# One layer of a streaming encoder on one core: x and its norm weight loaded in four column groups, cached keys loaded one set ahead, the conv state's output spread out

## The chip, the core and the metric

One core of a Trainium2 chip runs the whole program: TensorE (PE, with its weight loads as PEld), VectorE (DVE), ScalarE (ACT), GpSimd (POOL) and SyncE (SP), which issues most of the DMAs. POOL issues the others. The metric is the time of the program on the device in microseconds (us). Three runs of the kernel before took 3035.05, 3035.47 and 3037.78 us, median 3035.47.

## The reference

The program is one layer, applied to a prompt of 512 positions and a sample of 64 positions with 1024 cached ones. Model width is 2048, all in fp32.

```python
h = rmsnorm(x, norm_w) * (1.0 + scale[:, None]) + shift[:, None]
proj = h @ w_in                                   # 18032 columns, split into the parts below
conv_out, conv_new = causal_conv(qkv_a, conv_prev, w_conv)   # conv_new is an output: 3 rows x 6144
o_a, S_new = gated_delta_rule(qa, ka, va, g, beta, S0)       # 16 heads of 128
y_a = (rmsnorm(o_a, gdn_norm_w) * silu(z_a)) @ w_branch_a
o_b = sparse_attention(q_b, q_i, w_i, pos, K, V, KI, topk, rel_bias)  # 16 heads, 2 sets of keys
y_b = (o_b * silu(z_b)) @ w_branch_b
merged = sigmoid(gl_a) * y_a + sigmoid(gl_b) * y_b
x = x + gate[:, None] * (merged @ w_out)
y = rmsnorm(x, final_norm_w)                      # prompt and sample
```

For the sample, K and V are the cached keys and values (`cache_k`, `cache_v`, 1024 positions, 2 sets of 128 columns) followed by the new ones.

## The kernel before

The work is a stream of 189 tiles of 128 columns of a weight matrix (`plan`, line 1706): first the columns of `w_in`, then `w_branch_a`, `w_branch_b` and `w_out`. A tile is 96 products of 128x128 by 128x288: the activations and the weights are split into a high and a low part (`whi`, `wlo`; `hh` and `hl` for h, `ga`, `gb`, `mg` later), and hi·hi, hi·lo and lo·hi are summed, for two halves (288 columns each) of the 576 positions. Tile n's products first take the 64 with `whi`, then the 32 with `wlo` (`run_tile`, line 314). While tile n runs, ACT splits the weights of tile n+1, in four pieces at products 4, 14, 24 and 34; the low part is finished by a DMA that POOL issues (`wlo <- wraw`, it adds the raw weights to the negated high part). At product 84 SP issues the load of tile n+3's raw weights (`wraw`, 1 MB in rows of 512 bytes). There are two buffers each of `wraw`, `whi` and `wlo`, so that a load of `wraw` waits on SP for POOL's transfer out of the same buffer.

Between the products stands the rest of the work: attention, recurrence, transposes, each written as a generator. The planner (`Plan`, line 70) keeps an estimate of PE's time in ns (`self.pe`) while the program is written out. After each product `tick` steps every task whose due time has come. A `yield` says when a task is due again: a number is so many ns of PE's time from now, a list of tiles is when these are estimated to be ready, a tuple of a list and a number is that plus so many ns, `None` is at once; `wait` polls other tasks every 200 ns. The estimate only decides the order in which instructions are written. On the chip each engine takes its own instructions in that order, and waits at each for what it reads and for its buffer. So a PE instruction that waits holds all products behind it, and a DMA on SP's queue holds all DMAs behind it.

Three places matter here.
- `open_att` (line 1779) is called at the first tile of the queries (`qb0`). It closes the buffers of the recurrence and opens a pool in the same memory. It spawns `conv_out` (line 1310), which transposes the new conv state on PE (`nc`), copies it on DVE (`ncr`, two buffers) and stores it; `gate_vectors`, which loads `gada`, 256 KB in rows of 2 KB, over and over; and `kv_load(0)` (line 1323).
- `kv_load(n)` loads set n's keys and values: `KT` and `V` of the new positions, then 1024 cached values, and the cached keys in two parts of 512 (`kst`, one buffer, 256 KB in rows of 512 bytes), which PE transposes (`kcp`) and DVE copies (`KC`). Set 1 is loaded when head 8 of 16 begins (`qb_pre`, line 1446).
- `open_final` (line 1814) is called at the first tile of `w_out`. It loads x (4 MB for the prompt, 0.5 MB for the sample) and the final norm's weight (`fw`, 1 MB, spread over the partitions). The tiles' epilogue `wo_epi` scales the sums by the gate on ACT (`og`), and `out_cols` (line 1657) transposes them on PE (`yp`, `yq`, in two buffers of PSUM that all transposes share), adds them to x on DVE (`xf`), takes squares on ACT (`fscr`) and multiplies by `fw` on DVE.

Tiles are called by their order: `qb0` is the first one of the queries, `wo0` the first one of `w_out`, and `wlo174` is the low part for tile 174. All DVE, ACT, POOL and SP instructions go through the helper at line 58, products through line 221 and transposes through line 236.

Of the kernel before, what the change touches and what calls it, by code (L numbers as in the profile page):

```python
# [7 lines left out]
F32 = mybir.dt.float32  # L8
# [200 lines left out]
class Kern(Plan):  # L209
# [54 lines left out]
    def load(self, n):  # L264
        if n >= len(self.stream):
            return
        d = self.stream[n]
        m = d["m"] = sum(w for _, _, w in d["srcs"])
        raw = d["raw"] = self.wp.tile([128, 2048], F32, tag="wraw", name=f"wraw{n}")
        r3 = raw[:, :KO * m].rearrange("p (k m) -> p k m", m=m)  # L270
        at = 0
        for src, c, w in d["srcs"]:
            self.S.dma_start(r3[:, :, at:at + w], src[:, c:c + w].rearrange("(k p) m -> p k m", p=128))
            at += w
# [1035 lines left out]
    def conv_out(self):  # L1310
        o, p = self.o, self.p3
        f = self.newc.rearrange("p a b -> p (a b)")
        for g, name in enumerate(("prompt", "sample")):
            dst = o["new_conv_" + name].rearrange("l b j (m p) -> (l b j m) p", p=128)
            for a, n in ((0, 96), (96, 48)):
                pt = yield from self.tr(f"nc{g}{a}")
                self.T32(pt[:n, :128], f[:, 144 * g + a:144 * g + a + n])
                r = p.tile([128, 128], F32, tag="ncr", name=f"ncr{g}{a}")
                self.V.tensor_copy(r[:n], pt[:n, :128])
                yield [r]  # L1320
                self.S.dma_start(dst[a:a + n], r[:n])

    def kv_load(self, n):
        i, p, S = self.i, self.p3, self.S
        KT = p.tile([128, T], F32, tag="KT", name=f"KT{n}", bufs=1)
        S.dma_start(KT, self.d_kT[n])
        V = p.tile([128, 13, 128], F32, tag="V", name=f"V{n}", bufs=1)
        S.dma_start(V[:, 0:4, :], self.d_v[0:TP, 128 * n:128 * n + 128].rearrange("(t p) c -> p t c", p=128))
        S.dma_start(V[:64, 12, :], self.d_v[TP:T, 128 * n:128 * n + 128])
        S.dma_start(V[:, 4:12, :], i["cache_v"][0, 0, :, n, :].rearrange("(t p) c -> p t c", p=128))  # L1330
        KC = p.tile([128, PAST], F32, tag="KC", name=f"KC{n}", bufs=1)
        self.kvs = (KT, KC, V)
        for g in range(2):
            k = p.tile([128, 4, 128], F32, tag="kst", name=f"kst{n}{g}", bufs=1)
            S.dma_start(k, i["cache_k"][0, 0, 512 * g:512 * g + 512, n, :].rearrange("(t p) c -> p t c", p=128))
            yield [k]
            pt = yield from self.tr(f"kcp{n}{g}")
            for t in range(4):
                self.T32(pt[:, 128 * t:128 * t + 128], k[:, t, :])
            self.V.tensor_copy(KC[:, 512 * g:512 * g + 512], pt)  # L1340
            yield None
        yield [V, KT, KC]

    def attend(self, a):
# [9 lines left out]
    def attend_block(self, a, t, BT):  # L1354

        V, A, p, h = self.V, self.A, self.p3, a["h"]
        KT, KC, VV = self.kvs
        sc = 128 ** -0.5
# [5 lines left out]
        pl = yield from self.tp(f"lg{h}{t}")  # L1364
        self.mm(pl[:, :nk], a["qT"][:, q], KT[:, :nk])
        L = p.tile([128, nk], F32, tag=f"L{t}", name=f"L{h}{t}", bufs=1)
# [30 lines left out]
    def attend_sample(self, m):  # L1397
        V, A, S, p = self.V, self.A, self.S, self.p3
        KT, KC, VV = self.kvs
        sc = 128 ** -0.5  # L1400
# [238 lines left out]
    def wo_epi(self, j):  # L1639
# [14 lines left out]
                self.spawn(self.finish((0, 1), self.cols[KO - 2], self.cols[KO - 1]))  # L1654
        return epi

    def out_cols(self, j, g, ts):

        V, A, p, x = self.V, self.A, self.p8, self.x
        c = slice(128 * j, 128 * j + 128)  # L1660
        yield [g]
        full = [t for t in ts if t < 4]
        a, b = full[0], full[-1] + 1
        pt = yield from self.tr(f"yp{j}_{a}")
        for t in full:
            self.T32(pt[:, 128 * t:128 * t + 128], g[:, 128 * t:128 * t + 128])
        V.tensor_tensor(x[:, a:b, c], pt[:, 128 * a:128 * b].rearrange("p (a b) -> p a b", b=128), x[:, a:b, c], op=ALU.add)
        if 4 in ts:
            pt = yield from self.tr(f"yq{j}")
            self.T32(pt[:64, :128], g[:, TP:])  # L1670
            V.tensor_tensor(x[:64, 4, c], pt[:64, :128], x[:64, 4, c], op=ALU.add)
        yield 900
        for t in ts:
            n = 128 if t < 4 else 64
            scr = p.tile([128, 128], F32, tag="fscr", name=f"fscr{j}{t}")
            A.activation(scr[:n], x[:n, t, c], AF.Square, accum_out=self.sq[:n, t, j:j + 1])
        if j < KO - 1:
            yield 1500
            V.tensor_tensor(x[:, a:b, c], x[:, a:b, c], self.fw[:, c].unsqueeze(1).to_broadcast([128, b - a, 128]), op=ALU.mult)
            if 4 in ts:  # L1680
                V.tensor_tensor(x[:64, 4, c], x[:64, 4, c], self.fw[:64, c], op=ALU.mult)
# [132 lines left out]
    def open_final(self):  # L1814
        self.drain()
        self.cgb.close()
        self.c8, p = self.pool("p8", side="left")
        self.p8 = p
        i, S = self.i, self.S
        self.og, self.cols = {}, {}  # L1820
        self.x = p.tile([128, 5, D], F32, name="xf", bufs=1)
        S.dma_start(self.x[:, 0:4, :], i["x_prompt"][0].rearrange("(t p) d -> p t d", p=128))
        S.dma_start(self.x[:64, 4, :], i["x_sample"][0])
        self.fw = p.tile([128, D], F32, name="fw", bufs=1)
        S.dma_start(self.fw, i["final_norm_w"].partition_broadcast(128))
        self.sq = p.tile([128, 5, KO], F32, name="sqf", bufs=1)
        self.V.memset(self.sq[64:128, 4, :], 1.0)

# [113 lines left out]
```

## Time and profile before

| | |
|---|---|
| median of three runs | 3035.47 us |
| the profiled execution's own time | 3037.4 us |
| its span, first to last instruction | 3035.6 us |
| PE busy | 2938.0 us, 97% of the span |
| PEld busy | 2824.9 us, 93% |
| DVE, ACT, POOL busy | 40%, 50%, 13% |
| mean granted clock of TensorE | 0.986 of full speed |
| DMA, mean | 184 GB/s |

PE is busy nearly always, but the shares are a mean over stages. In the views by time a row begins with its start and its length in us; what stands in brackets at its end is how long the engine stood before it, and for what. A granted clock of 1.00 is the upper of TensorE's two levels (2.4 GHz), 0.50 the lower (1.2 GHz). q1 is the queue of SP's DMAs, q0 that of POOL's; after the name stand packets, MB, and the time that they took as a share of 16 DMA engines.

### The profile page before, as it was taken

To read this page: it belongs to the slowest core of one execution; us is meant where nothing else is said; L and a number is where in the kernel's file an instruction comes from. 1 tells how busy PE (TensorE), PEld (TensorE's weight loads), DVE (VectorE), ACT (ScalarE), POOL (GpSimd) and SP (SyncE) were. 2 spreads that over 40 slices of the span, in tenths; PEclk is the share of its full clock that TensorE was granted. 3 is DMA by queue.
4 is the path that set the end of the run, shared out by engine and by line. 5 is a ranking of instruction groups with operands and counts; after the bars stand their busy time and mean duration, and the time that the engine had idled before them with its cause. 6 is when DMAs were issued, how large, how long until landed. Compare 5 with 4: busy or idle time off the path is not lost.

```text
span 3035.6 us, 59288 instructions
## 1 busy us (share of the span) xinstructions
PE 2938.0 (97%) x23931; PEld 2824.9 (93%) x23931; DVE 1205.0 (40%) x3643; ACT 1531.8 (50%) x3428; POOL 399.3 (13%) x792
## 2 busy tenths in 40 slices
PE   5999999999999999999999999899999999999897
PEld 2599999999999999999999999899999999999897
DVE  3344896544454455544542434244322111112112
ACT  3266445555555555655554545354544443344454
POOL 1011111111111111111111111000111111111110
PEclk7999999999999999999999999999999999999999
DMA  9875887667677666767768677777679889888875
GB/s 326 273 162 125 188 191 183 158 161 177 154 164 168 157 161 155 172 163 173 168 158 191 164 165 179 177 168 167 151 171 263 231 223 225 217 204 213 217 160 139
DMA packets 571379, 558.84 MB, mean 184 GB/s; under 512 B 55121, under 2 KB 465650, under 8 KB 569890
## 3 DMA queue, kind: packets, MB, share of 16 engines
q1 hardware_dynamic: 515794, 354.69, 40.8%
q0 software_dynamic: 55168, 200.30, 34.5%
q8 instruction: 188, 3.08, 0.4%
q14 instruction: 85, 0.70, 0.1%
q10 hardware_dynamic: 144, 0.07, 0.0%
HBM read 313.52 MB, written 47.48 MB: 119 GB/s over the span
## 4 chain that ended last, share of the span: by engine, by line
PE 82%; DMA 10%; ACT 3%; DVE 2%; SPq 2%; issue 1%; POOL 0%; ACTq 0%; DVEq 0%; POOLq 0%
PE mm L221 66%; DMA yl<-d_ya 2%; SPq L58 2%; DMA za<-d_za 2%; DMA wlo<-wraw 1%; DMA wa<-in_w_ada 1%; DMA gbl<-d_gb 1%; PE ob L221 1%; PE lg L221 1%; PE ada L221 1%; PE po L221 1%; PE mmp L221 1%; PE dot L221 1%; DMA xf<-in_x_sample 1%; ACT wlo L58 1%
## 5 line engine op out<-in xcount | busy, mean ns | idle before, releaser
L221 PE MATMUL mm<-hh,whi 128*128 128x288 f32 (+1 forms) x4448 | 1223.8, 301 | 3.9 <-ACT gth L58 3.7
L221 PE MATMUL mm<-hl,whi 128*128 128x288 f32 (+1 forms) x4448 | 1221.2, 300 | 0.0
L221 PEld LDWEIGHTS mm<-hh,whi 128*128 128x128 f32 (+1 forms) x4448 | 838.0, 188 | 13.8 <-ACT gth L58 4.2
L221 PEld LDWEIGHTS mm<-hl,whi 128*128 128x128 f32 (+1 forms) x4448 | 838.4, 188 | 8.2 <-issue 3.8
L221 PE MATMUL mm<-hh,wlo 128*128 128x288 f32 (+1 forms) x4448 | 685.1, 302 | 0.0
L221 PEld LDWEIGHTS mm<-hh,wlo 128*128 128x128 f32 (+1 forms) x4448 | 615.4, 189 | 1.9 <-issue 0.9
L58 POOL DMA_DIRECT2D wlo<-wraw x376 | 323.2, 860 | 2231.9 <-ACT wlo L58 1875.4
L58 ACT ACTIVATE whi<-wraw 128x512 fp32r<-128x512 f32 x756 | 467.3, 618 | 96.9 <-DMA wraw<-in_w_branch_b 61.0
L58 ACT ACTIVATE wlo<-whi 128x512 fp32r<-128x512 f32 x752 | 475.2, 632 | 77.2 <-PE mm L221 37.3
L221 PE MATMUL mm<-ga,whi 128*128 128x288 f32 x1024 | 141.9, 299 | 8.2 <-DVE ta L58 8.2
L221 PEld LDWEIGHTS mm<-ga,whi 128*128 128x128 f32 x1024 | 139.5, 191 | 8.9 <-DVE ta L58 8.9
L221 PE MATMUL mm<-mg,whi 128*128 128x288 f32 x1024 | 144.0, 298 | 0.0
L221 PE MATMUL mm<-gb,whi 128*128 128x288 f32 x1024 | 139.9, 296 | 0.6 <-DVE tb L58 0.6
L221 PEld LDWEIGHTS mm<-mg,whi 128*128 128x128 f32 x1024 | 138.7, 189 | 0.0
L221 PEld LDWEIGHTS mm<-gb,whi 128*128 128x128 f32 x1024 | 137.5, 188 | 1.3 <-DVE tb L58 1.3
L58 DVE SCALAR_TENSOR_TENSOR cv<-raw,cw,cv 128x579 f32<-128x579 f32 x144 | 117.9, 818 | 27.8 <-ACT cv L58 24.2
L58 DVE SCALAR_TENSOR_TENSOR gacc<-gada,cs,gacc 128x512 f32<-128x512 f32 x120 | 86.2, 744 | 3.2 <-DMA gada<-in_w_ada 3.2
L58 ACT ACTIVATE raw<-mm 128x288 f32<-128x288 f32 x96 | 36.7, 382 | 82.9 <-PE mm L221 82.1
L58 ACT ACTIVATE gth<-mm 128x288 f32<-128x288 f32 x64 | 25.9, 407 | 103.7 <-PE mm L221 102.5
L58 ACT ACTIVATE x<-px 128x128 f32<-128x128 f32 x80 | 21.9, 273 | 107.7 <-PE px L221 107.7
L58 DVE TENSOR_TENSOR xf<-yp,xf 128x512 f32<-128x512 f32 (+1 forms) x18 | 11.4, 632 | 161.7 <-PE yp L236 134.0
L58 DVE SCALAR_TENSOR_TENSOR tb<-tb,mm 128x288 f32<-128x288 f32 x32 | 14.5, 453 | 144.3 <-DMA tb<-d_t 105.1
(494 smaller groups left out, 3437.8 us busy)
## 6 DMA issues: line engine op xcount, KB each, us to landing
wlo<-wraw POOLq DMA_DIRECT2D x376, 512.0 KB, 5.4
wraw<-in_w_in SPq DMA_DIRECT2D x140, 1024.0 KB
wa<-in_w_ada SPq DMA_DIRECT2D x64, 512.0 KB
gada<-in_w_ada SPq DMA_DIRECT2D x64, 256.0 KB
wraw<-in_w_branch_a SPq DMA_DIRECT2D x16, 1024.0 KB
wraw<-in_w_branch_b SPq DMA_DIRECT2D x16, 1024.0 KB
wraw<-in_w_out SPq DMA_DIRECT2D x16, 1024.0 KB
d_t<-gth SPq DMA_DIRECT2D x32, 288.0 KB
```

The costliest lines, as they stand in the source:

```text
L58: r = f(*a, **k)
L221: self.nc.tensor.matmul(out, lhsT, rhs, start=start, stop=stop, **k)
```

## The change

Three parts of the program are edited; nothing else differs.

1. `x_in` (new) loads x and `fw` in four groups of 512 columns. Group g waits until the task of group g-1 is done, which is 14 us of the planner's time after its loads were issued. `out_cols` for column tile j waits for the tasks of the groups before its own, and for every fourth tile its transposes are due 2 us later than before.
2. `kv_load` issues the load of the first cached keys before all its other loads, and that of the next part as soon as the one buffer is free, so that set 1's first part is loaded right after set 0's second. Transposes are due 4 us after the estimated landing, except for set 1's first part, which is due at once.
3. `conv_out` waits 24 us of the planner's time ahead of each of its four pieces.

```diff
@@ conv_out
             for a, n in ((0, 96), (96, 48)):
+                yield 24000
                 pt = yield from self.tr(f"nc{g}{a}")
@@ kv_load
+        def load(m, g):
+            k = p.tile([128, 4, 128], F32, tag="kst", name=f"kst{m}{g}", bufs=1)
+            S.dma_start(k, i["cache_k"][0, 0, 512 * g:512 * g + 512, m, :].rearrange("(t p) c -> p t c", p=128))
+            return k
+        k = load(0, 0) if n == 0 else self.kst
         KT = p.tile([128, T], F32, tag="KT", name=f"KT{n}", bufs=1)
...
         for g in range(2):
-            k = p.tile([128, 4, 128], F32, tag="kst", name=f"kst{n}{g}", bufs=1)
-            S.dma_start(k, i["cache_k"][0, 0, 512 * g:512 * g + 512, n, :].rearrange("(t p) c -> p t c", p=128))
-            yield [k]
+            yield [k], 4000 * (g or 1 - n)
...
             yield None
+            if n + g < 2:
+                k = self.kst = load(n + g, 1 - g)
@@ new
+    def x_in(self, g):
+
+        S, i, c = self.S, self.i, slice(512 * g, 512 * g + 512)
+        if g:
+            yield from self.wait(self.xl[g - 1])
+        S.dma_start(self.x[:, 0:4, c], i["x_prompt"][0][:, c].rearrange("(t p) d -> p t d", p=128))
+        S.dma_start(self.x[:64, 4, c], i["x_sample"][0][:, c])
+        S.dma_start(self.fw[:, c], i["final_norm_w"][c].partition_broadcast(128))
+        yield 14000
@@ out_cols
-        yield [g]
+        yield from self.wait(*self.xl[:j // 4])
+        yield [g], 0 if j % 4 else 2000
@@ open_final
-        S.dma_start(self.x[:, 0:4, :], i["x_prompt"][0].rearrange("(t p) d -> p t d", p=128))
-        S.dma_start(self.x[:64, 4, :], i["x_sample"][0])
         self.fw = p.tile([128, D], F32, name="fw", bufs=1)
-        S.dma_start(self.fw, i["final_norm_w"].partition_broadcast(128))
+        self.xl = []
+        for g in range(4):
+            self.xl.append(self.spawn(self.x_in(g)))
```

SP's queue where the first set of keys is loaded (`qb0`), before; `d_t` is the store of a gate tile, `kst01` the second part of set 0:

```order
L58 DMA d_t_85<-gth15_20000 128x576
L58 DMA gada0_20042<-in_w_ada 128x512
L58 DMA gada1_20044<-in_w_ada 128x512
L58 DMA KT0_20048<-d_kT_80 128x576
L58 DMA V0_20050<-d_v_81 128x4x128
L58 DMA V0_20050<-d_v_81 64x128
L58 DMA V0_20050<-in_cache_v 128x8x128
L58 DMA kst00_20055<-in_cache_k 128x4x128
L58 DMA out_new_conv_prompt<-ncr00_20040 96x128
```

The same place now:

```order
L58 DMA d_t_85<-gth15_20000 128x576
L58 DMA gada0_20038<-in_w_ada 128x512
L58 DMA gada1_20040<-in_w_ada 128x512
L58 DMA kst00_20044<-in_cache_k 128x4x128
L58 DMA KT0_20046<-d_kT_80 128x576
L58 DMA V0_20048<-d_v_81 128x4x128
L58 DMA V0_20048<-d_v_81 64x128
L58 DMA V0_20048<-in_cache_v 128x8x128
L58 DMA wraw98_20154<-in_w_in 128x16x128
L58 DMA kst01_20164<-in_cache_k 128x4x128
```

`kst00` has moved ahead of `KT0` and `V0`, the four conv stores are gone from here, and `kst01` follows the weight load.

PE at the end of that tile, before; the tile's 64 products with `whi` and the four `nc` transposes stand ahead of these rows:

```order
L221 MATMUL mm95_0_20036<-hh_105,wlo95_19887 128x288 x10
L236 MATMUL kcp00_0_20161<-ident_60,kst00_20055 128x128 x4
L221 MATMUL mm95_0_20036<-hh_105,wlo95_19887 128x288 x6
L221 MATMUL mm95_1_20113<-hh_105,wlo95_19887 128x288 x16
L221 MATMUL mm96_0_20202<-hh_105,whi96_20060 128x288
```

And now, with the 64 products alone ahead of them:

```order
L221 MATMUL mm95_0_20036<-hh_105,wlo95_19887 128x288 x16
L221 MATMUL mm95_1_20093<-hh_105,wlo95_19887 128x288 x5
L236 MATMUL kcp00_0_20157<-ident_60,kst00_20044 128x128 x4
L221 MATMUL mm95_1_20093<-hh_105,wlo95_19887 128x288 x11
L221 MATMUL mm96_0_20181<-hh_105,whi96_20056 128x288
```

The transposes of `kst00` have moved from behind 74 products of the tile to behind 85, and no `nc` is left in it. The transposes of `kst01` stand behind 70 products of the next tile, where before they stood behind 8.

SP's queue where the second set is loaded (`qb8`), before; the transposes of `kst10` stood behind 68 products of that tile, those of `kst11` behind 10 of the next:

```order
L58 DMA V1_23243<-in_cache_v 128x8x128
L58 DMA kst10_23248<-in_cache_k 128x4x128
L58 DMA gada36_23259<-in_w_ada 128x512
L58 DMA gada37_23330<-in_w_ada 128x512
L58 DMA kst11_23343<-in_cache_k 128x4x128
L58 DMA wraw116_23365<-in_w_in 128x16x128
```

And now:

```order
L58 DMA V1_23245<-in_cache_v 128x8x128
L58 DMA gada36_23258<-in_w_ada 128x512
L58 DMA kst11_23260<-in_cache_k 128x4x128
L58 DMA gada37_23338<-in_w_ada 128x512
L58 DMA wraw116_23365<-in_w_in 128x16x128
```

`kst10` is loaded with the first set, some 17 tiles earlier, and its transposes stand behind 2 products of the tile; `kst11` is one place behind where `kst10` was, and its transposes stand behind 7 products of the next tile.

SP's queue at the start of the last stage, before:

```order
L58 DMA wraw175_31678<-in_w_out 128x16x128
L58 DMA xf_31700<-in_x_prompt 128x4x2048
L58 DMA xf_31700<-in_x_sample 64x2048
L58 DMA fw_31703<-in_final_norm_w 128x2048
L58 DMA wraw176_31807<-in_w_out 128x16x128
```

And now, the first two of four groups:

```order
L58 DMA wraw175_31678<-in_w_out 128x16x128
L58 DMA xf_31700<-in_x_prompt 128x4x512
L58 DMA xf_31700<-in_x_sample 64x512
L58 DMA fw_31701<-in_final_norm_w 128x512
L58 DMA wraw176_31807<-in_w_out 128x16x128
L58 DMA xf_31700<-in_x_prompt 128x4x512
L58 DMA xf_31700<-in_x_sample 64x512
L58 DMA fw_31701<-in_final_norm_w 128x512
L58 DMA wraw177_31947<-in_w_out 128x16x128
```

Each of `wraw175` to `wraw178` is now followed by one group of three loads.

## Rows read from the trace of the kernel before

**Rows 1.** The chain that ended last, two clean tiles of `w_out`: start, length, what.

```profile
2861.51 12.73 PE mm L221 x96
2874.78 12.73 PE mm L221 x96
```

**Rows 2.** PE in order of time, first keys and conv output.

```profile
1619.22 0.30 PE L221 MATMUL mm<-hh,whi 128*128 128x288 f32 x1
...
1626.42 0.45 PE L236 MATMUL nc<-ident,newc 128*96 128x128 f32 x1 [4.82 <-DVE ncr L58]
...
1641.07 0.30 PE L221 MATMUL mm<-hh,whi 128*128 128x288 f32 x1
```

**Rows 3.** PE in order of time, second set of keys.

```profile
1931.31 0.40 PE L221 MATMUL mm<-hh,whi 128*128 128x288 f32 x1
...
1947.16 1.08 PE L236 MATMUL kcp<-ident,kst 128*128 128x128 f32 x4 [6.52 <-DMA kst<-in_cache_k]
...
1953.61 0.30 PE L221 MATMUL mm<-hh,whi 128*128 128x288 f32 x1
```

**Rows 4.** PE in order of time, start of the last stage.

```profile
2821.92 1.61 PE L221 MATMUL mm<-mg,whi 128*128 128x288 f32 x11
2832.52 1.11 PE L236 MATMUL yp<-ident,og 128*128 128x128 f32 x4 [8.99 <-ACT og L58]
...
2846.08 1.61 PE L221 MATMUL mm<-mg,whi 128*128 128x288 f32 x11
```

**Rows 5.** All engines in order of time, start of the last stage.

```profile
2800.07 1.56 SPq L58 DMA_DIRECT2D xf<-in_x_prompt  x1
...
2826.41 0.69 DVE L58 TENSOR_TENSOR xf<-yp,xf 128x512 f32<-128x512 f32 x1 [27.68 <-DMA xf<-in_x_prompt]
2827.13 0.31 ACT L58 ACTIVATE fscr<-xf 128x128 f32<-128x128 f32 x1 [15.26 <-DVE xf L58]
...
2844.15 0.50 ACT L58 ACTIVATE og<-mm,gate 128x288 f32<-128x288 f32 x1 [3.06 <-PE mm L221]
```

**Rows 6.** DMA queues from 2806 to 2814: packets, MB, share of 16 engines.

```profile
q1 hardware_dynamic: 213, 1.74, 53.9%
q0 software_dynamic: 212, 0.80, 50.2%
```

**Rows 7.** DMA queues from 1631 to 1632.

```profile
q1 hardware_dynamic: 209, 0.39, 104.2%
```

**Rows 8.** DMA queues from 2848 to 2901, clean tiles of `w_out`.

```profile
q0 software_dynamic: 1158, 4.20, 41.6%
q1 hardware_dynamic: 8481, 4.31, 30.4%
```

**Rows 9.** The chain that ended last, first keys and conv output.

```profile
1620.99 4.89 DMA d_t<-gth
```

**Rows 10.** SP's queue in order of time, first keys and conv output.

```profile
1625.94 0.81 SPq L58 DMA_DIRECT2D gada<-in_w_ada  x2
```

**Rows 11.** DMA queues from 1626 to 1631.

```profile
q0 software_dynamic: 226, 0.82, 88.9%
q1 hardware_dynamic: 131, 0.26, 15.1%
```

**Rows 12.** DMA queues from 1632 to 1633.

```profile
q1 hardware_dynamic: 461, 0.36, 107.3%
```

**Rows 13.** DMA queues from 1624 to 1626.

```profile
q1 hardware_dynamic: 201, 0.40, 51.3%
```

**Rows 14.** PE in order of time, two short waits.

```profile
2365.74 0.40 PE L221 MATMUL mm<-hh,whi 128*128 128x288 f32 x1 [2.27 <-ACT gth L58]
...
2477.84 2.53 PE L221 MATMUL mm<-ga,whi 128*128 128x288 f32 x9 [2.11 <-DVE ta L58]
```

**Rows 15.** By stretch, behind these waits: us, busy (x) of PE, PEld, DVE, ACT, POOL, clock, DMA.

```profile
2366.00:2370.00 4.00, 4.00 (x32) 4.00 (x32) 0.00 (x0) 0.00 (x0) 0.00 (x0) 1.00 0.51 103
2478.00:2481.00 3.00, 3.00 (x13) 3.00 (x14) 0.15 (x1) 2.90 (x6) 0.86 (x1) 0.50 1.07 373
```

## The prediction

> **What bounds the kernel now.** I read the page's engine shares first, then who PE waited for in the second half, then PE's own order of time at its three longest waits there, and last the queues around them. The page gives PE 97% of the span, so only time in which PE stands, or runs at the lower of its two clocks, can be won. Three of its four longest waits after 1600 us are these: a transpose nc waits 4.82 us for DVE's ncr [rows 2], kcp waits 6.52 us for the DMA of kst [rows 3], yp waits 8.99 us for ACT's og [rows 4]. They lie exactly at the change's three edits: the conv state's output, the cached keys, the last stage.
>
> What each costs in all is read as a distance between two tile starts, since that holds the clock's fall too. A clean tile of the last stage is 96 products and 5 transposes from start to start: 2874.78 - 2861.51 = 13.27 us, 12.73 us of it the products [rows 1]. So 96 products take about 12.8 us with the step to the next, one 0.133 us, and a transpose 0.1 us.
> - Place A, the conv output: the tile from 1619.22 to 1641.07 [rows 2] is 21.85 us long and holds 96 products and 8 transposes, 13.7 us. Lost: 8.2 us.
> - Place B, the second set of cached keys: from 1931.31 to 1953.61 [rows 3], 22.30 us against 12.8 + 0.4 = 13.2. Lost: 9.1 us.
> - Place C, the last stage: from 2821.92 to 2846.08 [rows 4], 24.16 us against 13.27. Lost: 10.9 us. Here DVE stood 27.68 us for x and ACT 15.26 us behind DVE [rows 5], and PE behind ACT.
> Together 28.2 us. All else that PE waits for in the second half is untouched by the change.
>
> **Place C, the last stage.** Before, one transfer of 4 MB, issued at 2800.07, reached DVE at 2826.41 [rows 5], because it shared the DMA engines packet by packet with the weights' accumulation: from 2806 to 2814 the SP queue moved 213 packets of 8 KB and POOL's queue 212 of 4 KB [rows 6]. Now the first group is 704 packets of 2 KB (512 of the prompt, 64 of the sample, 128 of the norm weight). Ahead of it stands wraw, as before. While POOL's 256 packets run, pairs of 2 + 4 KB take the place of 8 + 4 KB: 26.6 pairs per us [rows 6] become about twice as many, so 256 pairs take some 4.8 us; the other 448 packets go at the 209 per us that packets of 2 KB reached from 1631 to 1632 [rows 7], 2.1 us. From about 2805, when wraw's 1 MB is through, this ends near 2812, with the landing near 2813. The transposes for column 0 are put 17 products later (2.3 us), which costs PE nothing, and the squares on ACT now stand behind the whole next weight split. What ACT must not be late for is og of the tile: it starts 1.9 us before the tile's end (2844.15 [rows 5] against 2846.08 [rows 4]), so here at 2820.0. Five squares of 0.31 us [rows 5], each with a read of its sum, need about 2.5 us, so x may land until 2817.5. Slack 4.5 us: the wait goes, with its lower clock.
>
> The other three groups are due only at columns 4, 8 and 12, 53 us apart on PE, while the order puts one behind each weight load. They cost DMA time: from 2848 to 2901, four tiles of 13.25 us, the SP queue had 30.4% and POOL's 41.6% [rows 8], 4.0 and 5.5 us a tile; a group adds 704 / 209 = 3.4 us. Sum 12.9 of 13.27 us. It fits, barely, for four tiles, and weights are loaded nearly two tiles ahead. I charge 0.2 us. SP issues nine DMAs more, behind waits for POOL's transfers that it had anyway, and what stands behind them is a weight load due a tile later. Won at C: 10.7 us. Bounds: 0 (x still late) and 10.9.
>
> **Place A, the conv output and the first keys.** The four transposes nc move on, 24 us apart by the planner, and the wait for ncr goes: DVE's copy waited for the landing of d_t, 4.89 us after 1620.99 [rows 9]. What is late next is kst00. It is third on the SP queue now, behind two gada, but these wait for the same landing and start at 1625.94 [rows 10], as before. PE reaches kcp00 after 85 products, at 1619.22 + 11.3 = 1630.5. Until then 256 packets of gada (2 x 256 KB in rows of 2 KB) and kst00's own 512 (512 B each) must be through. From 1626 to 1631 the SP queue got 131 packets beside POOL's 226 [rows 11], then 209 and 461 in one us each [rows 7, 12]: 801 at 1633.0, so 768 a little before. From the last packet to the release I take 0.9 us (d_t's packets ended about 1625.0, half way through the two us of [rows 13], and released at 1625.88): 1633.8, and PE waits 3.3 us. The bounds are a wait of 0 (the keys' packets pass first) and one of 8, all that the tile lost before; I take 3.3, since the transfers ahead of the keys are the same as in these rows. Such a wait may drop the clock or not: after 2.11 us that ended at 2477.84 PE ran at 0.50, after 2.27 us that ended at 2365.74 it stayed at 1.00 [rows 14, 15]. Three us at half speed cost 1.5; I take half of that, 0.8. Won at A: 8.2 - 3.3 - 0.8 = 4.1 us.
>
> The Trainium skill (DMA: Bandwidth & Descriptors, "Queues, rings and completion order") says that each DMA engine changes between queues packet by packet and that a packet there is some 9 to 17 descriptors. By that several rows of 2 KB or 512 B would pass in one turn, the keys would be done about when POOL's 226 are, near 1631, and A would win 2.5 us more. The trace speaks against it: 131 to 226 is no more than one row to a turn [rows 11].
>
> The moved nc transposes keep their 0.1 us each; their copies wait only for PE, and their stores on SP stand behind loads that PE does not need next. kst01 now follows KT, V and wraw98 on the SP queue: from 1632.9 on 128 + 576 + 1024 + 2048 + 512 packets at 461 per us [rows 12] are 9.3 us, 1642.2. It is wanted 70 products into the next tile, which starts about 1636, so near 1645: no second wait, and at most 3 us if POOL's packets come between.
>
> **Place B, the second set of keys.** kst10 has been in SBUF for 300 us, so kcp10, now 2 products into the tile, waits for nothing. The wait goes to kst11: it takes kst10's place on the queue but one, behind gada36. kst10 came at 1947.1, when PE went on [rows 3]; 128 packets of gada more are 0.6 us: 1947.7. PE wants kcp11 103 products and 4 transposes after 1931.31, at 1945.5. Wait 2.2 us, and again 0.8 for the clock. SP issues kst11 behind a wait for kcp10 on PE, which is long past; gada37 and wraw116 behind it are wanted later. Won at B: 9.1 - 2.2 - 0.8 = 6.1 us. Bounds: 9.1 (kst11 is in time) and 0 (it comes as late for kcp11 as kst10 did for kcp10).
>
> **Sum.** 10.7 + 4.1 + 6.1 = 20.9 us. The profiled execution took 3037.4 us for a span of 3035.6; less 20.9 it would be 3016.5. The median of the three timed runs is 3035.5, 1.9 lower, so the forecast is 3014.6 us.
>
> **Rivals.**
> - *All three waits vanish.* For it: both waits on keys that I keep are a few us between two estimates, and one row's place in the queue decides them. Against: gada and keys cannot start before d_t has landed, and POOL's packets are then in front. Time: 3035.5 - 28.0 = 3007.5.
> - *The keys are as late as before.* Both waits only change their name, from ncr to kst00 and from kst10 to kst11, and the lower clock stays; for it speaks how little the SP queue gets while POOL's packets run [rows 11]; against it, that kst00 is now in front of 1,728 packets that it stood behind. Only C is won: 3024.8.
> - *The groups are too dear (slower).* If the transfers of a group cannot overlap, each costs what d_t's 288 KB took from issue to landing, 4.9 us [rows 9], so three take 14.7 us a tile; with 9.5 for the weights that is 24.2 against 13.27, late by 10.9 a tile in four tiles, 43.7, less one tile of lead, 30 us at C in place of the 10.9 lost before. With A and B won, 3035.5 - 10.2 - 10.9 + 30 = 3044. The sign turns at some 12.4 us a group. Against it: gada's transfers of 256 KB went back to back at 0.39 MB in one us [rows 7]. The Trainium skill (DMA: Bandwidth & Descriptors, "Rules for kernel authors") does say to gather small transfers into large ones; the same row shows no such price where the queue is full.
> - *Nothing is spaced.* The 14 us are the planner's time; on the chip a group only follows a weight load in SP's order. But column 0 needs the first group alone, so even bunched groups behind it give the forecast's time or go the third rival's way; no case of its own.
>
> **How the numbers follow.** The forecast as summed 0.62 (own range 3010 to 3019), all waits gone 0.16, keys late as before 0.14, groups too dear 0.04, a gain undone in a place that these rows don't show 0.04 (about 3035). The range of 3006 to 3024 holds the first two and leaves out about half of the third and the rest. A measurement of this kernel can tell some 0.2%, 6 us: the first three cases are faster by more, 0.92; within 0.2% 0.04; slower 0.04.
>
> **What would show it.** Right: in the first tiles of the last stage no wait of yp for og over 1 us and PE at full clock; in each of the two places of the keys a wait of kcp for kst of 2 to 4.5 us, and none for ncr. Wrong: x's first group landing later than 17.5 us after its issue, PE waiting for wlo in the four tiles with groups, or waits for the keys near 6 us or under 1.

## The result, and the profile after

The changed kernel took 3021.55 us, the median of four runs (3019.79 to 3023.28), beside 3036.62 us for the kernel before in the same comparison (3035.05 to 3045.5): ratio 0.9938, 95% interval 0.9922 to 0.9954. Measured again beside the experiments below it was 3021.93 us (six runs, 3016.20 to 3024.78), with 3038.68 before: ratio 0.9940, 0.9923 to 0.9956. So it is faster by 0.6%, some 18 us (18.8 and 18.2 by the ratios; the medians themselves stand 15.1 and 16.8 apart), and by more than the 0.2% that the forecast took as its bound. The forecast was 3014.6 us, 20.9 less than before.

The profiled execution took 3022.47 us, 14.9 less than that of before. PE is busy for the same 97% of the span as before. The rows below are read against those of before, place by place.

PE at place A, in order of time (start, length, what; in brackets how long PE stood, and for what); against [rows 2]:

```profile
1625.45 0.30 PE L221 MATMUL mm<-hh,whi 128*128 128x288 f32 x1
...
1639.79 0.63 PE L236 MATMUL kcp<-ident,kst 128*128 128x128 f32 x4 [2.85 <-DMA kst<-in_cache_k]
...
1642.36 0.45 PE L221 MATMUL mm<-hh,whi 128*128 128x288 f32 x1
```

The tile is 16.91 us long in place of 21.85. The wait for `ncr` is gone, and what is late next is `kst00`, as forecast, by 2.85 us. Behind it the products start 0.24 us apart for a while, not 0.13.

PE at place B, against [rows 3]:

```profile
1934.32 0.60 PE L236 MATMUL kcp<-ident,kst 128*128 128x128 f32 x4
...
1947.29 0.30 PE L221 MATMUL mm<-hh,whi 128*128 128x288 f32 x1
...
1949.75 0.66 PE L236 MATMUL kcp<-ident,kst 128*128 128x128 f32 x4 [1.37 <-DMA kst<-in_cache_k]
```

`kcp10` waits for nothing. `kcp11`, in the next tile, waits 1.37 us.

PE at place C, against [rows 4], and DVE, ACT and SP there, against [rows 5]:

```profile
2804.22 3.72 PE L221 MATMUL mm<-mg,whi 128*128 128x288 f32 x27
2807.78 0.60 PE L236 MATMUL yp<-ident,og 128*128 128x128 f32 x4
...
2817.50 1.61 PE L221 MATMUL mm<-mg,whi 128*128 128x288 f32 x11
...
2830.77 1.48 PE L221 MATMUL mm<-mg,whi 128*128 128x288 f32 x10
```

```profile
2794.87 1.79 SPq L58 DMA_DIRECT2D xf<-in_x_prompt  x1
...
2809.03 0.69 DVE L58 TENSOR_TENSOR xf<-yp,xf 128x512 f32<-128x512 f32 x1 [14.73 <-DMA xf<-in_x_prompt]
...
2820.63 0.63 ACT L58 ACTIVATE whi<-wraw 128x512 fp32r<-128x512 f32 x1 [2.28 <-DMA wraw<-in_w_out]
```

Each of the two tiles is a clean 13.27 to 13.28 us. The first group is there 14.2 us after its issue. The one trace of the crowding is ACT, which stood 2.28 us for the weights of tile 176, and that stays hidden: ACT is done with `og` and the split in time.

Clock and DMA share at the three places (stretch, length, busy (x) of PE, PEld, DVE, ACT, POOL, granted clock, DMA share, GB/s):

```profile
1641.00:1644.00 3.00, 3.00 (x14) 3.00 (x13) 1.69 (x4) 1.37 (x3) 0.00 (x0) 0.50 1.19 289
1946.00:1953.00 7.00, 5.63 (x43) 5.40 (x43) 3.50 (x6) 4.97 (x9) 0.98 (x2) 1.00 0.86 230
2817.00:2870.00 53.00, 53.00 (x405) 53.00 (x405) 7.06 (x16) 29.15 (x84) 6.89 (x8) 1.00 0.99 248
```

Behind the wait of 2.85 us the clock is at its lower level, behind the one of 1.37 at the upper. With the groups the DMA engines are at 0.99 over four tiles, and PE is busy for all of them.

**Where the time went.** PE's first product of a tile can be found in both traces. How much the distance between two such starts differs from the same distance before gives a ledger by stage (minus is won, us). Tiles are counted here by these starts from 0, which is two behind the numbers in the names: tile 93 is the one of place A (`qb0`, `mm95` in the order of instructions), 111 of B, 173 of C. In the trace of before the tiles 93 to 109 run from 1619.2 to 1910.9 us, 110 to 117 to 2055.2, 118 to 172 to 2821.9, and 173 to 175 to 2872.6. The rows are the experiments below, all with one profile each.

| kernel | first tile's start | tiles 0-92 | A 93-109 | B 110-117 | 118-172 | C 173-175 | rest | A+B+C |
|---|---|---|---|---|---|---|---|---|
| changed | +2.8 | +3.4 | -3.6 | -7.4 | +0.3 | -10.9 | +0.4 | -21.9 |
| changed, again | +0.7 | +0.7 | -3.6 | -7.1 | -1.2 | -10.9 | +0.4 | -21.6 |
| groups only | -0.3 | +2.6 | +0.3 | +0.1 | +7.1 | -10.9 | +0.3 | -10.5 |
| keys only | +3.0 | +1.2 | -0.8 | -6.9 | +5.2 | -7.1 | -0.1 | -14.8 |
| spread only | -0.1 | -0.3 | +1.7 | -0.8 | +3.8 | -0.7 | -0.1 | +0.2 |
| transposes later | +0.9 | -0.3 | -7.9 | -8.2 | +1.8 | -10.9 | +0.4 | -27.0 |
| bunched groups | -0.2 | -0.8 | -4.7 | -6.9 | +11.9 | -5.9 | +0.4 | -17.5 |
| later, not early | -1.2 | -0.7 | -8.2 | -9.1 | -0.5 | -10.9 | +0.3 | -28.2 |
| later, not spread | -1.7 | -1.9 | +0.4 | -4.5 | +4.8 | -10.9 | +0.4 | -15.0 |

The three places gave 21.9 us. What is missing to the 14.9 of the profiles came from stages in which every engine's instructions stand row for row as before: the first tile started 2.8 us later (151.63 against 148.83), and a product in the recurrence stood 2.5 us with the clock falling behind it. PE in order of time in the changed kernel:

```profile
151.63 0.38 PE L221 MATMUL mm<-hh,whi 128*112 128x288 f32 x1 [0.21 <-ACT kvTk L58]
...
641.09 0.74 PE L221 MATMUL u<-TT,e 32*32 32x32 f32 x36 [2.50 <-DMA TT<-d_D]
...
2351.76 0.61 PE L221 MATMUL mm<-hh,whi 128*128 128x288 f32 x1 [6.83 <-ACT gth L58]
```

The third row is in the stage from 2300 to 2540 us, where loads come one by one to DVE and ACT and PE waits for ACT's `gth` or DVE's `ta` somewhere in every trace. Before, these waits were 3.7 and 8.2 us in all, here 7.2 and 4.9, with other tiles hit.

### The profile page after: what moved, and what is told of

Same layout as the page of the kernel before. It is cut to its first block, busy times and chain, and to the rows that moved or that the text cites. A ratio compares the mean times of both kernels' runs of the same rounds, so it can differ in the third digit from the quotient of the medians.

```text
span 3020.7 us, 59300 instructions
## 1 busy us (share of the span) xinstructions
PE 2937.3 (97%) x23931; PEld 2822.8 (93%) x23931; DVE 1205.1 (40%) x3643; ACT 1533.1 (51%) x3428; POOL 399.6 (13%) x792
## 4 chain that ended last, share of the span: by engine, by line
PE 86%; DMA 7%; DVE 2%; ACT 2%; SPq 1%; issue 1%; ACTq 0%; POOL 0%; DVEq 0%; POOLq 0%
PE mm L221 72%; DMA wa<-in_w_ada 2%; DMA za<-d_za 2%; DMA gbl<-d_gb 1%; SPq L58 1%; PE ob L221 1%; PE lg L221 1%; PE po L221 1%; PE dot L221 1%; PE ada L221 1%; PE mmp L221 1%; PE y L221 1%; PE px L221 1%; PE pT L236 1%; DMA kst<-in_cache_k 1%
## 5 line engine op out<-in xcount | busy, mean ns | idle before, releaser
L221 PEld LDWEIGHTS mm<-hh,whi 128*128 128x128 f32 (+1 forms) x4448 | 839.0, 189 | 17.5 <-ACT gth L58 7.7
L58 ACT ACTIVATE x<-px 128x128 f32<-128x128 f32 x80 | 21.9, 274 | 107.6 <-PE px L221 107.5
L221 PE MATMUL mm<-gb,wlo 128*128 128x288 f32 x512 | 70.8, 296 | 0.0
```

What stands on the lines that cost most here:

```text
L58: r = f(*a, **k)
L221: self.nc.tensor.matmul(out, lhsT, rhs, start=start, stop=stop, **k)
```

## The experiments

Eight runs, seven other kernels and the changed one again, each timed beside the kernel before on the same chip: the first four on one chip, the last four on another.

**Groups only.** Part 1 of the change alone:

```diff
 before + x_in, out_cols, open_final of the change
 (conv_out and kv_load as before)
```

> The column groups alone; keys and conv output as before. Ledger theory (each place is worth what its tile lost): only place C is won, 10.9 us, time about 10.9 under the kernel before, and no wait of yp for og over 1 us; places A and B keep tiles of about 21.9 and 22.3 us. Rival (a part of the gain at C is given back behind it, since the groups crowd the weights): less than 8 us. On the 6 us by which the changed kernel won less than its three places together: if they are chance in stages that the change does not touch, the start of the first tile and the tile near 640 us scatter by some us here, though their instructions are those of before; if the change causes them, the first tile starts 2.8 us later than before here too.

Measured: ratio 0.9971 (0.9958 to 0.9984), 8.8 us of 3037.78. PE's waits in the profile, from 1600 to 2000 and from 2780 to 2880 us (engine, for whom; total, times, longest):

```profile
PE kcp L236 <- DMA kst<-in_cache_k: 6.3, 1, 6.3
PE nc L236 <- DVE ncr L58: 5.5, 1, 5.5
...
PE mm L221 <- ACT mg L58: 1.4, 1, 1.4
```

A and B are as before, `yp` waits for nothing, and C is won whole: 10.9 us. The interval (4.9 to 12.8 us) holds the ledger's figure and the rival's too; what speaks against the rival is that nothing is given back behind C (+0.3, all of it behind the start of the last tile). The first tile was not late here (-0.3), so its 2.8 us above were not the groups'. All stages but the three lost 9.7 us in this profile, which was the slowest of the kernel's 12 runs (3036.6; median 3030.76).

**Keys only.** Part 2 alone:

```diff
 before + kv_load of the change
 (conv_out, x_in, out_cols, open_final as before)
```

> The early keys alone; conv output and last stage as before. Ledger theory: place B is won as in the changed kernel, 7.4 us; at place A nothing or under 1 us, because the first nc still waits 4.8 us for ncr and the clock falls behind it, and kst00 is then in time: the wait of kcp00 is 0. Time about 8 under before. Rival (the edits at A add up): A gives some 2 us, half of the 3.9 of the changed kernel, time about 9.5 under before.

Measured: ratio 0.9979 (0.9966 to 0.9992), 6.4 us. PE's waits at the three places:

```profile
PE nc L236 <- DVE ncr L58: 4.8, 1, 4.8
PE kcp L236 <- DMA kst<-in_cache_k: 1.9, 1, 1.9
...
PE yp L236 <- ACT og L58: 2.0, 1, 2.0
PE mm L221 <- ACT mg L58: 1.7, 1, 1.7
```

B is won (6.9), A gives 0.8: `nc` still holds PE 4.8 us. That is the ledger theory; the rival wanted 2 at A. The times do not tell the two apart (8 and 9.5 us under before; the interval is 2.4 to 10.3). A surprise stands in the last two rows. x is loaded in one piece here, as before, yet `yp` waits 2.0 us and not 9.0. A chance wait for `mg` two tiles earlier had cost PE some 4 us, and x came 22.6 us after its issue, not 26.3, so it was earlier against PE. So the stall at C is not of one size from run to run.

**Spread only.** Part 3 alone:

```diff
 for a, n in ((0, 96), (96, 48)):
+    yield 24000
     pt = yield from self.tr(f"nc{g}{a}")
```

> The spread conv output alone; keys and last stage as before. Ledger theory: the wait only changes its name. kcp00 stands behind 78 products, wanted some 10.5 us into the tile, and kst00 lands behind V about 17.8 us into it: a wait of 7.3 us and a lower clock behind it, so A loses 8 to 10 us as before, and the time is that of before within 3 us. Rival (the edits at A add up): some 2 us won.

Measured: ratio 1.0009 (0.9999 to 1.0019), 2.7 us slower by the ratio, within the 3 expected, and 4.5 by the medians; the interval also holds no change. PE at place A:

```profile
1636.84 1.09 PE L236 MATMUL kcp<-ident,kst 128*128 128x128 f32 x4 [7.42 <-DMA kst<-in_cache_k]
```

7.42 us against 7.3 expected. The wait only changed its name, and A lost 1.7 more than before. At A neither edit alone wins (-0.8 and +1.7), both together win 3.6: the two waits lie behind the same landing of `d_t`, and one covers the other.

**Transposes later.** The changed kernel with one number raised:

```diff
-            yield [k], 4000 * (g or 1 - n)
+            yield [k], 9000 * (g or 1 - n)
```

> The changed kernel with the keys' transposes due 9 us behind the estimated landing in place of 4. Ledger theory: the waits of kcp00 (2.85 us, with a lower clock behind it, 4.3 in all) and kcp11 (1.37 us, 1.7 in all) go, head 0 starts half a tile later at no cost, and the time is 6 us under the changed kernel, 21 under before. Rival (the wait moves to head 0's logits or to kst01, which is now loaded later): no gain, within 2 us of the changed kernel, with a wait of lg or kcp01 of 3 us or more in the trace.

Measured: ratio 0.9925 (0.9908 to 0.9943). PE's waits from 1600 to 2000:

```profile
PE obs L221 <- ACT PTs L58: 1.5, 3, 0.7
PE lg L221 <- DVE L L58: 0.9, 2, 0.8
```

No wait for keys is left, and no other came in its place: the three places give 27.0 us, 5.1 more than the changed kernel. The timed medians stand 4.3 to 4.6 apart, in the expected direction; the intervals of the two ratios overlap, so the size of this gain rests on the ledger.

**The changed kernel again.**

> The changed kernel itself once more, beside kernels that differ from it in one edit, on the same chip. Ledger theory: tile of A 4.9 shorter than before and the next 1.0 longer, B 9.0 shorter and the next 1.6 longer, C 10.9 shorter, as in its first profile; first tile and the tile near 640 us within 2 us of before if their loss there was chance, and then the time is 3 us lower against before than in the first measurement, some 18 under. If the loss belongs to the change, the first tile is late by 2.8 and the tile near 640 by 3.7 again, and the time is 15 under before.

The three places repeat to 0.3 us (-21.9 and -21.6), the waits of `kcp` are 2.82 and 1.65 us. The first tile (+0.7) and the tile near 640 (no wait over 1 us there) are not late: that loss was chance. This execution took 3016.41 us. Yet the median of its six runs is 3021.93, 18 under before by the ratio and not 21. The 18 are what was expected, but not that they would be 3 us more than in the first measurement: the ratio gave 18.8 there.

**Bunched groups.** The changed kernel without the spacing:

```diff
-        yield 14000
+        yield 0
```

> The changed kernel with all four column groups issued at once, ahead of the weights of tile 176: the spacing alone is undone. Theory (column 0 needs the first group alone, the rest only crowds): C's tile 13.3 us as in the changed kernel; but three x groups hold SP some 18 us ahead of the weight load, so the weights of tile 176 land some 5 to 10 us later than in the changed kernel, where ACT already waited 2.3 us for them, and PE waits 0 to 6 us for whi or wlo in one tile; time 0 to 6 us above the changed kernel. Rival (spacing is what wins at C): x is as late as before, a wait of yp for og near 9 us, 11 us above.

Measured: ratio 0.9955 (0.9938 to 0.9972); median 3024.40, 2.5 above the changed kernel, intervals overlapping. SP, ACT and PE in order of time:

```profile
2813.38 0.35 SPq L58 DMA_DIRECT2D fw<-in_final_norm_w  x1
2814.11 0.37 SPq L58 DMA_DIRECT2D wraw<-in_w_out  x1
```

```profile
2832.40 0.63 ACT L58 ACTIVATE whi<-wraw 128x512 fp32r<-128x512 f32 x1 [10.34 <-DMA wraw<-in_w_out]
```

```profile
2839.15 1.03 PE L236 MATMUL yp<-ident,og 128*128 128x128 f32 x4 [3.05 <-ACT og L58]
```

x is in time, as the theory said, but the weights of tile 176 (the number in `wraw`'s name) stand behind three more groups on SP's queue and are issued at 2814.11, in the changed kernel at 2808.76. ACT stands 10.34 us for them, is late with `og`, and PE stands 3.05 us with a lower clock behind it; the wait was expected for `whi` or `wlo` themselves. C gives 5.9 in place of 10.9. The four groups win 6 by being groups, and the spacing saves 5 more. The rival, x as late as before, is out. The large loss of this profile between B and C (+11.9) is not the edit's: 8.9 of it came before 2540 us, and 3.8 go to a wait for `mg`, behind a load from `d_t` for which DVE had stood 13.0 us until 2794.28, ahead of the first group's issue at 2794.57. Its A and B are the changed kernel's, with -4.7 and -6.9 where that had -3.6 and -7.4: in this execution `kcp` waited 2.86 us at A, and the clock stayed up behind it:

```profile
1633.00:1636.00 3.00, 3.00 (x25) 3.00 (x24) 2.23 (x4) 1.26 (x3) 0.00 (x0) 1.00 1.18 283
```

**Later, not early.** Groups and spread as in the change, keys loaded where they were before, transposes later:

```diff
 kv_load of the kernel before, with
-            yield [k]
+            yield [k], 9000
```

> Groups and spread as in the changed kernel, but the cached keys loaded where the kernel before loads them; only their transposes are due 9 us behind the estimated landing. It asks whether the early loads are worth anything. Theory (what is won at A and B is that PE asks later): kcp00 stands 55 products into the next tile, some 20.5 us from the tile's start, and kst00 lands some 17.8 us into it; kcp10 is asked for some 19 us after its tile's start and lands 15.8 us into it: no wait of kcp over 0.5 us, time 4 to 7 us under the changed kernel, as with early loads and late transposes together. Rival (the early loads are needed, since the second part comes late or head 0 and head 8 wait for keys): waits of kcp or lg of 3 us and more, time at or above the changed kernel.

Measured: median 3011.01 (3007.24 to 3018.17, five runs), ratio 0.9908 (0.9891 to 0.9926). The page of this profile puts PE at 98%. PE's transposes of the keys, in order of time:

```profile
1637.52 0.60 PE L236 MATMUL kcp<-ident,kst 128*128 128x128 f32 x4
...
1652.47 0.60 PE L236 MATMUL kcp<-ident,kst 128*128 128x128 f32 x4
...
1940.23 0.60 PE L236 MATMUL kcp<-ident,kst 128*128 128x128 f32 x4
...
1954.80 0.60 PE L236 MATMUL kcp<-ident,kst 128*128 128x128 f32 x4
```

Not one of the four waits. The places give 28.2 us, against 27.0 with the early loads and 21.9 in the changed kernel: 6.3 under the latter by the ledger, within the 4 to 7 expected, and 10.9 by the medians. So the early loads were not needed: PE only had to ask later. By its median it is the fastest kernel here, below the changed one by 0.3% (the intervals overlap from 0.9923 to 0.9926).

**Later, not spread.**

```diff
 the kernel of "Transposes later" (9000), and in conv_out
-                yield 24000
```

> The changed kernel with transposes of keys due 9 us behind the landing, and the conv output not spread. Theory (nc waits for ncr, ncr for the landing of d_t, whatever becomes of the keys): nc waits 4.8 to 5.5 us at A with a lower clock behind it, A loses 7.5 to 8.5 us more than with the spread, time some 8 above the kernel with spread and late transposes. Rival (once the keys are late, A has slack and the nc wait is small): under 2 us.

Measured: median 3028.47, ratio 0.9964 (0.9951 to 0.9976). PE's waits from 1600 to 2000:

```profile
PE nc L236 <- DVE ncr L58: 5.0, 1, 5.0
PE lg L221 <- DVE L L58: 3.4, 3, 2.9
```

`nc` waits 5.0 us whatever becomes of the keys, and A is where it was before (+0.4 against -7.9 with the spread): 8.3 us, as expected. The time is some 12 us above that of "Transposes later" by the two ratios, where 8 were expected. The further 3.7 at B belong to a wait of `lg` for DVE that the other kernels do not have; why it falls on this one is open.

## Why the prediction was right, point by point

- **Place C (10.7 forecast, 10.9 measured, in six profiles with spaced groups).** Right in mechanism and size. The first group landed 14.2 us after its issue; 12.9 was forecast, and 17.5 the limit. The four groups were charged 0.2 us and cost PE nothing in their tiles, though DMA was at 0.99; behind the start of the last tile the profiles with groups are 0.3 to 0.4 us longer than before, those without 0.1 shorter. What of this the 2 us do by which the transposes of column 0 were put later was not tried apart.
- **Place A (4.1 forecast, 3.6 measured).** Right in mechanism and in its working: `kst00` is late next. Its wait was put at 3.3 us and was 2.85. The forecast gave SP's queue 131 packets beside 226 of POOL's in the five us behind the issue of `gada` [rows 11], then 209 and 461. Behind the issue at 1632.32 the queues show this (packets, MB, share), first the five us from 1632.38, then 1637.38 to 1638.38, then 1638.38 to 1639.38:

```profile
q0 software_dynamic: 220, 0.77, 87.5%
q1 hardware_dynamic: 150, 0.29, 15.8%
```

```profile
q1 hardware_dynamic: 391, 0.37, 104.7%
```

```profile
q1 hardware_dynamic: 402, 0.38, 112.6%
```

  So the 768 packets were through near 1639.0, and the keys were there 7.5 us after the issue (1632.32 to 1639.79), where 7.9 was forecast. That the queues change turns with several rows each, as the forecast weighed it from the Trainium skill (DMA: Bandwidth & Descriptors, "Queues, rings and completion order"), gets no support here either: 150 packets beside 220. The clock behind the wait was charged at 0.8, half of what a fall was thought to cost, and cost some 1.7 (8.2 lost before, less 3.6 won, less 2.85 of wait). Behind the wait of 2.86 us in the bunched kernel it did not fall, so a price between none and the whole was fair.
- **Place B (6.1 forecast, 7.1 to 7.4 measured).** The wait went to `kcp11`, 1.37 and 1.65 us where 2.2 was forecast. The 0.8 for the clock was too much: it stayed at 1.00. The forecast had wanted 2 to 4.5 us at each of the two places as the sign of being right and under 1 as that of being wrong; B lies between.
- **The sum (20.9 forecast, 21.9 and 21.6 at the places).** The three terms hold within 1.3 us each.
- **The time (3014.6 forecast, 3021.55 and 3021.93 measured).** It lies in the stated range, but above the case's own range (3010 to 3019), and by time alone it stands between that case and *keys as late as before* (3024.8); what tells these apart are the waits at the places. What missed is the last step, "The profiled execution took 3037.4 us for a span of 3035.6; less 20.9 it would be 3016.5": it carries everything outside the three places over unchanged from one profile. The profiled execution took 3022.47 us, 6.0 more: 7.0 were lost outside the places, and 1.0 more was won at them. The last 1.0 is the way from the profile to the median, 1.9 in the forecast and 0.9 here. The stages outside the places move by several us from run to run with the same instructions: their sums in the nine profiles lie between -2.1 and +11.3 us of before's. Some of the win is also smaller in some executions of before: where a chance wait for `mg` falls just ahead of C, x comes earlier against PE, and the tile of C has only 3.8 us to give (keys only, 17.02 us long). That wait is in three of the ten profiles, which would take some 2 us off the mean win, an estimate from these profiles. The ratios stand for 18.8 and 18.2 us, and their intervals (14.0 to 23.7 and 13.4 to 23.4) hold both the forecast's 20.9 and the ledger's 21.9 and 21.6. So it is open whether a difference of 3 us between ledger and ratios is there at all, and what makes it up.
- **The rivals.** *All waits vanish* (3007.5): not so here, but raising one number brought it about (27.0 us at the places). *Keys as late as before*: out, with waits of 2.85 and 1.37. *Groups too dear*: out as they are spaced. *Nothing is spaced* was dismissed with the words "even bunched groups behind it give the forecast's time or go the third rival's way", and that was wrong: bunched they go a middle way, x in time and the next weights late, 5 us at C by one profile. The argument looked at column 0 and the DMA engines' load, not at who stands behind the groups on SP.

## What to carry to other kernels

When a wait is to be moved, list everything that hangs on the same landing: here neither edit at A won alone, because the conv transposes and the keys both stood behind one store, and each hid the other. Where the consumer's place in its engine's order is free, asking 5 us later cost nothing here, and did what loading earlier did not do alone. Cut a large load into the pieces its consumers need, and put the later pieces where no nearer load stands behind them in the issuing queue.

## What the runs showed that was not expected

- Waits of 2.82 and 2.85 us of PE were followed by some 3.4 us at the lower clock (0.50), and one of 2.86 at the same place (bunched groups) was not; waits of 1.37 and 1.65 us in the changed kernel were not. But 1.70 us for `mg` and 0.39 more just behind it (keys only) were. So in these rows the length of a wait alone does not tell what the clock does.
- How long SP holds one load at its issue varies much, and not with its size: an x group's prompt part took 1.79 us as the first in the changed kernel and 0.43 as the third of the bunched ones; the next sample part, an eighth of its size, took 5.60. What sets it was not tried.
- A fixed program scatters by more than its single edits are worth: the kernel before ran from 3029.66 to 3048.61 us in 29 runs on one chip. The ledger by tile starts names the place of an edit of 5 us from one profile, where the medians' intervals overlap. But a place scatters too, by 1.1 us at A with the same instructions, and once by 7.1 at C with nothing edited there (keys only): the row of the wait has to be read beside it.
